# A hand-fixed instruction order for the recurrence preparation of a hybrid decoder layer

## The chip, the core and the metric

The kernel runs on one core of one Trainium2 chip. A core has a matmul engine (TensorE, PE in the profile, with PEld for its weight loads), three engines for element-wise work (VectorE or DVE, ScalarE or ACT, GpSimd or POOL), and a queue for transfers (SyncE or SP). ACT and POOL can also issue transfers, in line with their other instructions. Each engine works through its own list of instructions in order; engines wait for each other by semaphores. The metric is the device time in microseconds (us) of one execution; a kernel's time is the median of its runs.

## The reference

One decoder layer on x of 1024 tokens by 1024 features, all in fp32:

```python
h = rms_norm(x, norm1_g)
proj = h @ w_in
p_rwkv, p_sb, q_mem, gate_logits = jnp.split(proj, cut, axis=-1)
y_a = rwkv7_branch(p_rwkv, ...)      # token shift, delta-rule recurrence, group norm, bonus
y_b = stick_breaking_branch(p_sb, ...)
y_m = memory_branch(q_mem, mem, ...)
merged = sum over branches of sigmoid(gates) * (branch @ w_branch)
x = x + merged @ w_out
x = x + conv_ffn(x, ...)
```

The part that the change touches is the start of `rwkv7_branch`: a token shift `p + (prev - p) * mu` of each projected tile, and what the recurrence needs per head before its steps can be done in chunks of 64 tokens:

```python
a = sigmoid(a0 + al @ a2);  g = sigmoid(gl) @ g2
kk = k * k_k / max(norm(k * k_k), 1e-12)
k  = k * (1 + (a - 1) * k_a)
S  = S * w + (S @ -kk) (kk * a)^T + v k^T;   y = S @ r
bonus = sum(r * k * r_k) * v
y = (group_norm(y) + bonus) * g
```

## The kernel before

Every large product is taken as three matmuls of fp32r halves (a high part and the rest), `mm3`: high times high, high times low, low times high. The work is written as Python generators. `stream` yields the *filler*: one item for each 128 columns of a projection. An item (`shift_item`, L286 to L299) fetches its weight tile on SP (`wr`, L77), splits it on ACT (`wh`, L81) and POOL (`wl`, L82) one item ahead, and then does eight steps, one for each 128 rows of the input; a step is six matmuls into two PSUM banks of the tag `mm`. At the end of an item `shifted` (L240 to L250) does the token shift: a memset and two multiplications by the row norm on VectorE (L244, L246, which read the two banks), a scaling on ACT (L247), and the weighted sum on VectorE (L249). `settle` marks the finished tile in the fourth step of the next item.

`rwkv_prep(p, ...)` prepares two of the eight heads for the recurrence, p = 0 to 3. `weave` alternates: one step of the preparation, up to its next `yield`, then one step of the filler. So the list of PE's instructions is fixed by the code: `pinned` ties each matmul and transpose behind the instruction that was written before it on its engine. VectorE's, ACT's and POOL's instructions in the preparation are not tied before the change. A scheduler puts them in order by its own estimate of when they are ready; instructions of the preparation are given a higher priority than the filler.

In the order of the code, a preparation of the kernel before is: the two low-rank gates (L320, L321 on ACT), a scan (L330) and kp (L326) on VectorE; the sums of squares on PE, a maximum (L335), a power on POOL (L337) and its spread over a tile `ex` (L255); rk (L353); the transposes of v with their copies (L359) and four stores from ACT; the transposes of `ex` on PE and kk (L369), b (L370); `chain(0)`; the bonus products of `blk` and rk on PE with `bon` on VectorE (L429, L430) and the scaling of g on ACT (L432); `gram` for the first and second quarter; `chain(1)`; `turned(0)`; `gram` for the third and fourth quarter; `turned(1)`. `chain(h)` makes the operands of half h: four products with 64 partitions (L379, two with b and two with kp) and three instructions for `ra` (L380, L381, L382). `gram(h, f)` is 16 matmuls with 64 rows each into two banks, and two multiplications by a mask on VectorE that empty them (L396). `decayed(h)` (POOL, L408) scales half h, `turned(h)` transposes that on PE (L106), and ACT copies the result (L418). All these banks are of the tag `g`, of which there are four.

After the four preparations the filler goes on with the projections of the second branch. `differ` (L681) subtracts two tiles on VectorE four times; one tile of each comes back from memory, where it was stored just before. `inst` (L452, a transfer issued by POOL) loads what the Gram groups stored in `mad`, for `inverse`, which runs on VectorE in the stage after.

Of the kernel before, what the change touches and what calls it, by code (L numbers as in the profile page):

```python
# [50 lines left out]
class Trunk:  # L51
    def __init__(self, ctx, tc, I, out):
        self.ctx, self.tc, self.nc, self.I, self.out = ctx, tc, tc.nc, I, out
        self.uid = 0
        self.pin = False
# [52 lines left out]
    def pinned(self, ins):  # L108
        if self.pin:
            self.tc.keep_in_program_order(ins)  # L110

# [128 lines left out]
    def shifted(self, ti, tag, pp=None):  # L240
        nc = self.nc
        pp = pp or self.proj(self.I["w_in"][ti])
        pr, tmp = self.t4(), self.t4()
        nc.vector.memset(tmp[:, 0:1], 0.0)  # L244
        for h in range(2):
            nc.vector.tensor_tensor(pr[:, h * 512 : (h + 1) * 512], pp[h], self.rbc[:, h * 512 : (h + 1) * 512], ALU.mult)  # L246
        nc.scalar.activation(tmp[:, 1:1024], pr[:, 0:1023], AF.Copy, scale=self.par("mu", ti))  # L247
        out = self.t4(tag)
        nc.vector.scalar_tensor_tensor(out, pr, self.omm[:, ti : ti + 1], tmp, ALU.mult, ALU.add)  # L249
        return out  # L250

    def expand_heads(self, f, tag="w4"):
        nc = self.nc
        ex = self.t4(tag)
        nc.vector.tensor_copy(  # L255
            ex[:, :1024].rearrange("p (j h i) -> p j h i", j=8, h=2),
            f.rearrange("p (j h) -> p j h", j=8).unsqueeze(3).to_broadcast([128, 8, 2, 64]),
        )
        return ex
# [26 lines left out]
    def shift_item(self, ti, out, name):  # L286
# [18 lines left out]
    def rwkv_prep(self, p, krv, need):  # L305
# [3 lines left out]
        halves = [slice(0, 512), slice(512, 1024)]  # L309
        if p == 0:  # L310
# [5 lines left out]
        for hs in halves:  # L316
# [3 lines left out]
            nc.scalar.activation(a[:, hs], pa, AF.Sigmoid, bias=self.par("a0", p))  # L320
            nc.scalar.activation(su[:, hs], pu, AF.Sigmoid, bias=self.par("w0", p))  # L321
        P = self.t4("qk")
        nc.scalar.activation(P, k, AF.Square, scale=self.par("k_k", p))
        kp = self.t4("qk")
        nc.scalar.activation(kp, a, AF.Identity, scale=self.par("k_a", p), bias=self.omka[:, p : p + 1])
        nc.vector.tensor_tensor(kp, k, kp, ALU.mult)  # L326
        for _ in range(2):
            yield
        cc = Q = su
        nc.vector.tensor_tensor_scan(cc, self.seg, su, 0.0, ALU.mult, ALU.add)  # L330
        for _ in range(2):
            yield
        pst = self.head_ss(P)
        mx = self.small("rs", [128, 16])
        nc.vector.tensor_scalar(mx, pst, 1e-24, None, ALU.max)  # L335
# [3 lines left out]
        for hs in halves:  # L339
            pgh = self.ps("g")  # L340
            self.mmul(pgh, lora[:, 512 + p * 128 : 512 + (p + 1) * 128], self.sg[:, hs], start=True, stop=True)
            nc.scalar.activation(g[:, hs], pgh, AF.Copy)
        nc.scalar.activation(P, cc, AF.Exp, scale=-EXPM, bias=self.offs[:, 0:1])
        pc = self.pc[p]
        nc.scalar.activation(pc, cc.rearrange("p (c s) -> p c s", c=NC)[:, :, 63], AF.Exp, scale=-EXPM)
        nc.scalar.activation(Q, cc, AF.Exp, scale=EXPM, bias=self.offs[:, 1:2])
        ex = self.expand_heads(inv, "it")
        for _ in range(3):
            yield
        need(f"v{p}")  # L350
        r, v = krv[1], krv[2]
        rk = self.t4("qk")
        nc.vector.scalar_tensor_tensor(rk, r, self.par("r_k", p), kp, ALU.mult, ALU.mult)  # L353
        vt = self.t4("qk")
        for h, hs in enumerate(halves):
# [3 lines left out]
            nc.scalar.activation(vt[:, hs], pt, AF.Copy)  # L359
# [5 lines left out]
        for _ in range(2):  # L365
            yield
        kk, b = k, a
        for hs, bc in zip(halves, self.bcast_heads(ex)):
            nc.vector.scalar_tensor_tensor(kk[:, hs], k[:, hs], self.par("k_k", p), bc, ALU.mult, ALU.mult)  # L369
        nc.vector.tensor_tensor(b, kk, a, ALU.mult)  # L370

        def chain(h):
            hs = halves[h]
            bk, ra = self.t4("qk"), self.t4("qk")
            bk4, ra4 = (x.rearrange("p (c u s) -> p c u s", c=8, u=2) for x in (bk, ra))
            for x, first in ((b, 1), (kp, 0)):
                for h2 in range(2):
                    q = slice(h2 * 64, h2 * 64 + 64)
                    nc.vector.tensor_tensor(bk4[q, :, first ^ h2], self.c8(x[q, hs]), self.c8(Q[q, hs]), ALU.mult)  # L379
            nc.vector.tensor_tensor(ra4[:, :, 0], self.c8(r[:, hs]), self.c8(P[:, hs]), ALU.mult)  # L380
            nc.vector.scalar_tensor_tensor(ra4[:, :, 1, 1:64], self.c8(P[:, hs])[:, :, 0:63], -1.0, self.c8(kk[:, hs])[:, :, 1:64], ALU.mult, ALU.mult)  # L381
            nc.vector.tensor_scalar(ra4[:, :, 1, 0], self.c8(kk[:, hs])[:, :, 0], -math.exp(OFF), None, ALU.mult)  # L382
            self.spill(p, h, 0, ra, nc.sync)
            return bk, ra

        def gram(h, f, bk, ra):
            mt = self.t4("at")
            mt4 = mt.rearrange("p (c h t) -> p c h t", c=4, h=2)
            pm = [self.ps("g"), self.ps("g")]
            for c in range(4):  # L390
                o = (f * 4 + c) * 128
                for h2 in range(2):
                    q = slice(h2 * 64, h2 * 64 + 64)
                    self.mmul(pm[h2][:, c * 128 : (c + 1) * 128], bk[q, o : o + 128], ra[q, o : o + 128], start=True, stop=True)
            for h2 in range(2):
                nc.vector.tensor_tensor(  # L396
                    mt4[:, :, h2], pm[h2].rearrange("p (c t) -> p c t", c=4),
                    self.mm_mask.unsqueeze(1).to_broadcast([128, 4, 128]), ALU.mult)
            g0 = h * 4 + f * 2
            nc.sync.dma_start(  # L400
# [1540 lines left out]
```

## Time and profile before

| what | us |
|---|---|
| median of 3 runs | 1829.22 (1829.06 to 1833.78) |
| the profiled execution | 1831.78 |
| its span from first to last instruction | 1830.0 |
| PE busy in the span | 1785.9 (98%) |
| VectorE busy | 1191.1 (65%) |
| ACT busy | 881.9 (48%) |
| POOL busy | 771.2 (42%) |
| granted TensorE clock, mean | 0.995 |

Matmuls overlap, so that a matmul's own length in the profile (about 0.39 us for 512 columns) is longer than the distance between the starts of two. Distances are the better measure of what PE does. Idle time of PE is what the waits of PE add up to; idle time of another engine costs something only where PE waits for it in the end. The four preparations lie between 60 and 286 us of the span.

### The profile page before, as it was taken

What the parts mean: (1) busy time and instruction counts of PE and PEld (TensorE: products, weight loads), DVE (VectorE), ACT (ScalarE), POOL (GpSimd) and SP (SyncE); (2) the same over time, 40 slices, a digit from 0 to 9 for tenths busy, and PEclk for the clock granted to TensorE, in tenths of its full rate; (3) what the DMA queues carried; (4) which work ended last, traced back from release to release, by engine and by line L of the source; (5) the groups of instructions that cost most, each with busy time, mean ns of one, the idle gap of its engine ahead of it and who ended that gap; (6) DMA issues with size and microseconds to landing.
All of it is one profiled execution on the core that took longest, in us unless ns stands there. A gap on an engine that the chain in (4) does not pass through costs nothing.

```text
span 1830.0 us, 27430 instructions
## 1 busy us (share of the span) xinstructions
PE 1785.9 (98%) x10468; PEld 1445.7 (79%) x10468; DVE 1191.1 (65%) x1659; ACT 881.9 (48%) x1665; POOL 771.2 (42%) x441
## 2 busy tenths in 40 slices
PE   8999999999999999999899999989999999999999
PEld 6777778878788888787677878868888888888887
DVE  5657664988987514333444793597776777785497
ACT  5443342564666635534456443464454444545443
POOL 2322343232222452122233341376776767645454
PEclk9999999999999999999899999999999999999999
DMA  4255466111112351467665463323232232386475
GB/s 181 58 173 184 151 201 204 50 41 52 56 45 84 112 144 53 164 211 257 222 244 185 163 251 104 114 70 115 101 117 88 95 118 104 123 291 247 144 236 202
DMA packets 120613, 263.39 MB, mean 144 GB/s; under 512 B 28313, under 2 KB 40857, under 8 KB 120354
## 3 DMA queue, kind: packets, MB, share of 16 engines
q1 hardware_dynamic: 82722, 194.76, 32.6%
q10 hardware_dynamic: 33984, 54.27, 8.1%
q0 software_dynamic: 3776, 12.62, 2.2%
q8 instruction: 82, 1.34, 0.3%
q14 instruction: 49, 0.40, 0.1%
HBM read 180.04 MB, written 81.53 MB: 143 GB/s over the span
## 4 chain that ended last, share of the span: by engine, by line
PE 83%; DVE 8%; issue 3%; ACT 3%; POOL 2%; DMA 1%; ACTq 0%; SPq 0%; DVEq 0%; POOLq 0%
PE mm L113 67%; PE g L113 12%; PE g L106 3%; POOL dw L1677 1%; DVE qk L379 1%; DVE qk L381 1%; DVE it L462 1%; DVE BT L1318 1%; DVE inst L464 0%; DVE at L854 0%; DVE mg L1232 0%; DMA w<-yd 0%; ACT wh L81 0%; POOL wl L82 0%; DVE qk L382 0%
## 5 line engine op out<-in xcount | busy, mean ns | idle before, releaser
L82 POOL TENSOR_TENSOR wl<-wr,wh 128x1024 fp32r<-128x1024 f32 x77 | 196.8, 2557 | 473.4 <-ACT wh L81 469.7
L113 PE MATMUL mm<-xhi,wh 128*128 128x512 f32 x784 | 264.6, 418 | 9.4 <-ACT xhi L182 7.5
L113 PE MATMUL mm<-xlo,wh 128*128 128x512 f32 x784 | 245.8, 395 | 0.9 <-DVE xlo L183 0.9
L113 PE MATMUL mm<-xhi,wl 128*128 128x512 f32 x784 | 244.3, 393 | 0.3 <-POOL wl L82 0.2
L113 PEld LDWEIGHTS mm<-xlo,wh 128*128 128x128 f32 x784 | 148.8, 190 | 34.5 <-DVE xlo L183 1.6
L113 PEld LDWEIGHTS mm<-xhi,wl 128*128 128x128 f32 x784 | 148.3, 189 | 34.0 <-POOL wl L82 1.2
L113 PEld LDWEIGHTS mm<-xhi,wh 128*128 128x128 f32 x784 | 137.7, 191 | 39.5 <-issue 9.1
L81 ACT ACTIVATE wh<-wr 128x1024 fp32r<-128x1024 f32 x77 | 81.4, 1058 | 147.0 <-PE mm L113 85.4
L113 PE MATMUL mm<-dw,da 128*128 128x512 f32 x528 | 121.2, 390 | 0.0
L113 PE MATMUL mm<-BT,l 128*128 128x512 f32 x504 | 117.7, 390 | 0.0
L113 PEld LDWEIGHTS mm<-dw,da 128*128 128x128 f32 x528 | 99.0, 188 | 21.6 <-DVE da L1676 1.2
L1677 POOL TENSOR_TENSOR dw<-draw,dw 128x512 fp32r<-128x512 f32 x55 | 81.9, 1499 | 79.1 <-ACT dw L1675 76.4
L113 PE MATMUL mm<-BT,wh 128*128 128x512 f32 x352 | 109.2, 391 | 2.9 <-DVE BT L1318 2.9
L854 DVE TENSOR_TENSOR_SCAN at<-at,at 128x128 f32<-128x128 f32 (+3 forms) x64 | 93.4, 1460 | 26.6 <-ACT at L848 26.4
L113 PEld LDWEIGHTS mm<-BT,l 128*128 128x128 f32 x504 | 94.7, 188 | 19.6
L113 PE MATMUL mm<-B,wh 128*128 128x512 f32 x352 | 108.7, 390 | 1.5 <-DVE p L1508 1.5
L1676 DVE TENSOR_TENSOR da<-draw,da 128x512 fp32r<-128x512 f32 x77 | 67.0, 877 | 49.5 <-ACT da L1674 49.1
L1409 POOL TENSOR_TENSOR l<-it,l 128x1024 fp32r<-128x1024 f32 x21 | 51.6, 2458 | 95.5 <-ACT l L1408 95.5
L113 PE MATMUL g<-dw,da 128*128 128x512 f32 x396 | 90.6, 390 | 0.3 <-POOL dw L1677 0.3
L1674 ACT ACTIVATE da<-draw 128x512 fp32r<-128x512 f32 x77 | 48.3, 628 | 80.8 <-PE mm L113 30.9
L113 PEld LDWEIGHTS g<-dw,da 128*128 128x128 f32 x396 | 74.3, 188 | 16.1 <-POOL dw L1677 0.8
L756 DVE TENSOR_TENSOR w<-w,rbc 128x1024 f32<-128x1024 f32 x24 | 49.8, 2074 | 56.8 <-ACT w L755 55.0
(329 smaller groups left out, 3996.5 us busy)
## 6 DMA issues: line engine op xcount, KB each, us to landing
wr<-in_w_in_dram SPq DMA_DIRECT2D x50, 512.0 KB, 3.6
draw<-actd SPq DMA_DIRECT2D x77, 256.0 KB, 3.5
at<-scr SPq DMA_DIRECT2D x28, 512.0 KB, 5.8
draw<-in_w_down_dram SPq DMA_DIRECT2D x55, 256.0 KB, 4.7
rw<-in_w_up_dram SPq DMA_DIRECT2D x22, 512.0 KB, 3.5
actd<-gall ACTq DMA_DIRECT2D x44, 256.0 KB, 3.3
gsd<-w ACTq DMA_DIRECT2D x20, 512.0 KB, 2.8
wr<-in_w_up_dram SPq DMA_DIRECT2D x20, 512.0 KB, 3.6
```

The source lines that it names most:

```text
L81: self.nc.scalar.activation(hi, raw, AF.Copy)
L82: self.nc.gpsimd.tensor_tensor(lo, raw, hi.bitcast(F32), ALU.subtract)
L106: self.pinned(self.nc.tensor.transpose(out, in_, self.ident[:n, :n]))
L113: self.pinned(self.nc.tensor.matmul(*a, **k))
L379: nc.vector.tensor_tensor(bk4[q, :, first ^ h2], self.c8(x[q, hs]), self.c8(Q[q, hs]), ALU.mult)
L381: nc.vector.scalar_tensor_tensor(ra4[:, :, 1, 1:64], self.c8(P[:, hs])[:, :, 0:63], -1.0, self.c8(kk[:, hs])[:, :, 1:64], ALU.mult, ALU.mult)
L756: nc.vector.tensor_tensor(g, g, self.rbc, ALU.mult)
L854: self.pinned(nc.vector.tensor_tensor_scan(sn[:, :W][:, ::-1], sn[:, :W][:, ::-1], self.smask[:, 1024 - W :][:, ::-1], 1.0, ALU.mult, ALU. ...
L1409: keep(eng.tensor_tensor(lo, src, hi.bitcast(F32), ALU.subtract))
L1674: self.pinned(nc.scalar.activation(A[:, 0], a, AF.Copy))
L1676: self.pinned(nc.vector.tensor_tensor(A[:, 1], a, A[:, 0].bitcast(F32), ALU.subtract))
L1677: nc.gpsimd.tensor_tensor(Wt[:, 1], w, Wt[:, 0].bitcast(F32), ALU.subtract)
```

## The change

**A fixed order.** While the four preparations are woven, `strict` is set. Each pinned instruction is then tied behind the last pinned one of its engine, in addition to the instruction written directly before it. And far more is pinned: all of the preparation's VectorE and ACT instructions but those of `decayed` and the power on POOL, and the token shifts of the filler. Not pinned are the weight splits, the transfers, `differ`, and the copies of the third projection group on ACT (L661).

**Shifts in two steps.** The last instruction of a token shift (L249) is put aside in `tails` and written in the second step of the next item, after whatever the preparation has written by then.

**VectorE's work piece by piece.** In the new order a preparation has 28 steps (27 before), numbered s0 to s27 here:

- s0 gates on PE and ACT; s2 scan; s3 kp; s4 sums of squares on PE, maximum, power on POOL, g and the three exponentials on ACT; s7 `ex`
- s8 transposes of v, copies, four stores from ACT, rk; s10 transposes of `ex` *and* the four bonus products on PE in one run, kk; s11 b
- s12 `ra` of half 0 and its store; s13 the two products with b; s14 the two with kp; s15 `decayed(0)`, the two `bon` multiplications; s16 the last `bon` step, the scaling of g, their stores
- s17 all 32 matmuls of `gram(0)` in one run, masks of the first quarter; s18 masks of the second quarter
- s19 `ra` of half 1; s20 `turned(0)`, products with b; s21 products with kp; s22 `decayed(1)`
- s24 all 32 matmuls of `gram(1)`, masks; s25 masks; s27 `turned(1)` and the load of `inst`

Before, all of kk, b and `chain(0)` were one step, and `chain(1)` was written together with the second `gram`. The four banks of the tag `g` are all taken in s10 (two for `ex`, two for the bonus, which are read in s10 and s15) and again in s17 and s24.

The core of the diff:

```diff
     def pinned(self, ins):
         if self.pin:
             self.tc.keep_in_program_order(ins)
+            if self.strict:
+                self.behind(ins, self.last_fixed.get(ins.ins.engine))
+            self.last_fixed[ins.ins.engine] = ins
+        return ins
...
     def shifted(self, ti, tag, pp=None):
...
+        finish = lambda: self.pinned(nc.vector.scalar_tensor_tensor(out, pr, self.omm[:, ti : ti + 1], tmp, ALU.mult, ALU.add))
+        if self.pin:
+            self.tails.append(finish)
...
     def shift_item(self, ti, out, name):
...
-            if k == 3:
+            if k == 1:
+                self.finish_tails()
+            elif k == 3:
                 self.settle()
...
+        bcs = self.bcast_heads(ex)
+        pbs = []
+        for hs in halves:
+            pbs.append(self.ps("g"))
+            self.mmul(pbs[-1], self.blk, rk[:, hs], start=True, stop=True)
+        for hs, bc in zip(halves, bcs):
+            stt(kk[:, hs], k[:, hs], self.par("k_k", p), bc, ALU.mult, ALU.mult)
+        yield
+        tt(b, kk, a, ALU.mult)
+        yield
...
+        def gram(h, bk, ra):
+            pms = []
+            for f in range(2):
+                pm = [self.ps("g"), self.ps("g")]
+                for c in range(4):
...
+                pms.append(pm)
+            for f, pm in enumerate(pms):
...
+                    tt(mt4[:, :, h2], pm[h2].rearrange("p (c t) -> p c t", c=4),
+                       self.mm_mask.unsqueeze(1).to_broadcast([128, 4, 128]), ALU.mult)
...
+                yield
...
+        self.strict = True
         for p in range(4):
             self.weave(self.rwkv_prep(p, krv[p], need), pump, 1.0)
+        self.strict = False
```

More of the change, by code (lines that the diff above doesn't have):

```diff
@@ L54, in __init__ @@
         self.uid = 0
-        self.pin = False
+        self.pin = self.strict = False
+        self.last_fixed, self.tails = {}, []
     def nm(self, s):
@@ L110, in pinned, with behind @@
             self.tc.keep_in_program_order(ins)
+            if self.strict:
+                self.behind(ins, self.last_fixed.get(ins.ins.engine))
+            self.last_fixed[ins.ins.engine] = ins
+        return ins
+    def behind(self, ins, prev):
+        if prev is not None:
+            self.tc.add_manual_dep(
+                ins.ins, prev.ins.name,
+                mybir.DependencyInfo(mybir.DependencyClass.NoSync, mybir.DependencyReason.DATA), reason="fixed order")
     def mmul(self, *a, **k):
@@ L258, in expand_heads @@
         )
+        if tag == "it":
+            self.pinned(ins)
         return ex
@@ L383, in chain @@
[L383 to L391, printed above, removed]
-                for h2 in range(2):
[L393 to L400, printed above, removed]
-                self.scr[p, g0 : g0 + 2, :, 512:1024].rearrange("g q c -> q g c"), mt.rearrange("q (g c) -> q g c", g=2))
-            for h2 in range(2):
-                i0 = p * 32 + h2 * 16 + h * 8 + f * 4
-                nc.sync.dma_start(self.mad[i0 : i0 + 4].rearrange("c s t -> s c t"), mt4[64 - h2 * 64 : 128 - h2 * 64, :, h2, 64:128])
+                    tt(bk4[q, :, first ^ h2], self.c8(x[q, hs]), self.c8(Q[q, hs]), ALU.mult)
@@ L665, in item @@
                         self.raw.append(raw)
-                if i == 1:
+                if i == 0:
+                    self.finish_tails()
+                elif i == 1:
                     self.settle()
```

133 lines of the change are left out of this document (74 added, 59 removed).

## The prediction

> **What bounds the kernel now.** I read the page first, then busy time by stage, then PE's waits in the stage that is touched, then the timeline around one of them.
>
> ```profile
> span 1830.0 us, 27430 instructions
> PE 1785.9 (98%) x10468; PEld 1445.7 (79%) x10468; DVE 1191.1 (65%) x1659; ACT 881.9 (48%) x1665; POOL 771.2 (42%) x441
> PE 83%; DVE 8%; issue 3%; ACT 3%; POOL 2%; DMA 1%; ACTq 0%; SPq 0%; DVEq 0%; POOLq 0%
> ```
>
> PE sets the time: 98% busy, and 83% of the chain that ended last. Only two things can move it: fewer waits of PE, and less time of PE itself. A window over the four preparations shows how much there is (busy us and instructions of PE, PEld, DVE, ACT, POOL, then clock, transfer share and rate):
>
> ```profile
> 60.00:286.00 226.00, 216.77 (x1243) 166.48 (x1242) 150.53 (x177) 90.33 (x111) 76.80 (x34) 0.99 0.52 166
> ```
>
> PE idles 226 - 216.8 = 9.2 us there, and VectorE is busy for two thirds of it, so it is not full on average. The waits of PE from 60 to 330 us name the cause:
>
> ```profile
> PE g L106 <- DVE at L396: 6.4, 3, 2.6
> PE g L113 <- DVE qk L382: 2.4, 2, 1.8
> PE g L106 <- DVE at L249: 0.4, 1, 0.4
> ```
>
> The largest is `turned(0)`, which needs a bank that the masks of the first Gram groups (L396) must empty. PE's and VectorE's timeline around the first of the three (start, length, then idle before):
>
> ```profile
> 93.27 0.61 PE L113 MATMUL mm<-xhi,wl 128*128 128x512 f32 x2
> 93.82 1.16 PE L113 MATMUL g<-qk,qk 64*128 64x128 f32 x16
> 94.91 0.73 PE L113 MATMUL mm<-xhi,wh 128*128 128x512 f32 x2
> 95.48 0.63 PE L113 MATMUL mm<-xlo,wh 128*128 128x512 f32 x2
> 98.63 0.62 PE L113 MATMUL mm<-xhi,wl 128*128 128x512 f32 x2
> 100.01 0.62 PE L113 MATMUL mm<-xhi,wl 128*128 128x512 f32 x2
> 102.89 1.16 PE L106 MATMUL g<-kon,it 128*128 128x128 f32 x8 [2.26 <-DVE at L396]
> ```
>
> ```profile
> 97.68 0.69 DVE L380 TENSOR_TENSOR qk<-at,qk 128x512 f32<-128x512 f32 x1
> 98.29 0.68 DVE L381 SCALAR_TENSOR_TENSOR qk<-qk,at 128x504 f32<-128x504 f32 x1
> 98.88 0.17 DVE L382 TENSOR_SCALAR qk<-at 128x8 f32<-128x8 f32 x1
> 100.86 1.29 DVE L249 SCALAR_TENSOR_TENSOR at<-w,omm,w 128x1024 f32<-128x1024 f32 x1 [1.21 <-ACT w L247]
> 102.06 2.48 DVE L396 TENSOR_TENSOR at<-g,kon 128x512 f32<-128x512 f32 x4
> ```
>
> The first Gram group was in its banks at 95.0. Its masks begin at 102.06, 7 us later, behind all of `chain(1)`, a token shift, and 1.21 us in which VectorE waits for ACT in that shift. So the wait is one of order and not of load.
>
> **The change, part by part.** Lengths of VectorE's instructions are means over 60 to 330 us (count, busy us, mean ns, idle before):
>
> ```profile
> L379 DVE TENSOR_TENSOR qk<-qk,qk 64x512 f32<-64x512 f32 x32 | 21.9, 684 | 0.5
> L396 DVE TENSOR_TENSOR at<-g,kon 128x512 f32<-128x512 f32 x32 | 20.1, 680 | 5.9 <-PE g L113 5.9
> L249 DVE SCALAR_TENSOR_TENSOR at<-w,omm,w 128x1024 f32<-128x1024 f32 x11 | 19.6, 1781 | 10.8 <-ACT w L247 10.8
> L246 DVE TENSOR_TENSOR w<-mm,rbc 128x512 f32<-128x512 f32 x22 | 14.2, 684 | 12.3 <-PE mm L113 12.2
> L381 DVE SCALAR_TENSOR_TENSOR qk<-qk,at 128x504 f32<-128x504 f32 x8 | 13.5, 1681 | 0.0
> L380 DVE TENSOR_TENSOR qk<-at,qk 128x512 f32<-128x512 f32 x8 | 8.4, 1044 | 0.2
> L382 DVE TENSOR_SCALAR qk<-at 128x8 f32<-128x8 f32 x8 | 5.7, 714 | 0.0
> L369 DVE SCALAR_TENSOR_TENSOR at<-at,params,g 128x512 f32<-128x512 f32 x8 | 5.6, 745 | 4.8 <-PE g L106 4.7
> L429 DVE TENSOR_TENSOR at<-g,at 128x512 f32<-128x512 f32 x8 | 5.4, 682 | 0.1
> L430 DVE SCALAR_TENSOR_TENSOR at<-at,params,qk 128x1024 f32<-128x1024 f32 x4 | 5.1, 1272 | 0.0
> L370 DVE TENSOR_TENSOR qk<-at,qk 128x1024 f32<-128x1024 f32 x4 | 4.9, 1225 | 0.1
> ```
>
> *(1) The old waits go: -9.2 us.* The masks now stand ahead of `chain(1)` and ahead of the next token shift, and the shift's last step stands two filler steps after ACT's scaling, so the 10.8 us before L249 go too. What is late next comes under (3) to (5).
>
> *(2) Gram groups of a half: -3.2 us.* A filler step of six matmuls takes 1.38 us (98.63 to 100.01), so two take 0.46. From 93.27 to 95.48 are four of them (0.92 us) and one Gram group, which thus takes 1.29 us: eight pairs side by side, 128 columns wide. The nearest run of eight at full rows is `turned(1)`:
>
> ```profile
> 117.03 0.62 PE L113 MATMUL mm<-xhi,wl 128*128 128x512 f32 x2
> 118.83 0.62 PE L113 MATMUL mm<-xlo,wh 128*128 128x512 f32 x2
> ```
>
> Eight transposes of 128 columns and four matmuls lie between these starts, so the transposes take 1.80 - 0.92 = 0.88 us. The other 0.41 us of a Gram group is for going into 64 rows and out. Eight such passages fall away: 8 x 0.4 = 3.2. Low end: only the visible edges, 0.09 us before 93.82 (93.27 + 0.46 = 93.73) and 0.11 us too much from 94.91 to 95.48, which is 0.2 x 8 = 1.6. I take the upper end, since width and count are alike. The bonus products were in one step already and have full rows; I cost their move at nothing on PE, bounds 0 and -0.8 (four passages at 0.2).
>
> *(3) A new wait before `gram(0)`: +4.4 us.* Filler items end every eighth step. Preparation 0 starts after six steps and waits in s8 for the mark of v0 (step 20); the others follow each 28 steps. So an item ends after s11 and s19 in preparations 0 and 2, after s7, s15 and s23 in 1, and 3 has no token shifts. In 0 and 2 VectorE now cannot go on with `ra` before PE has finished that item. From there PE has five filler steps to s17: 6.9 us. VectorE has L246 twice (1.37), `ra` (1.68 + 0.71 + 1.04 = 3.43), b products (1.37), the put-aside L249 (1.78), kp products (1.37): 9.3 us by the means. Where nothing disturbs it, `ra` takes 0.68 + 0.17 + 0.69 = 1.54 and L249 1.29 (timeline above): 6.9 us. The first quarter waits 0 to 2.4 us; the second also needs the bonus banks, whose two L429 take 1.36 against 0.9 of matmuls: 0.5 more. So 0.5 to 2.9 us, twice. What disturbs is POOL:
>
> ```profile
> 89.66 2.84 POOL L82 TENSOR_TENSOR wl<-wr,wh 128x1024 fp32r<-128x1024 f32 x1
> 90.18 2.87 DVE L381 SCALAR_TENSOR_TENSOR qk<-qk,at 128x504 f32<-128x504 f32 x1
> ```
>
> L381 needs 2.87 us beside the weight split and 0.68 us without. The next split becomes possible when an item ends, so one falls into this window; I take 2.2 us for each, 4.4 in all (ends 1.0 and 5.8). [...] In 1 and 3, from the transposes of `ex` on, VectorE needs kk (1.49), b (1.23), `ra` 3.43 and four products (2.74), 8.9 us, while PE has seven steps (9.7 us) and the bonus products, 1.9 us a preparation by this row:
>
> ```profile
> L113 PE MATMUL g<-qk,kon 128*128 128x512 f32 x16 | 7.5, 592 | 0.0
> ```
>
> No wait there. rk, which PE now needs in s10, is written two steps earlier; the slack is 2.8 us plus 1.8 us of transposes.
>
> *(4) `gram(1)`: +0.6 us.* From the end of the bonus reads to s24 PE has half a group (1.0), seven steps (9.7) and eight transposes (0.9): 11.6 us. VectorE has L430 (1.27), four masks (2.72), `ra` 3.43, four products 2.74, one L246 pair 1.37: 11.5. Level by the means; one more meeting with POOL (2.2 us) would show in one of three. Ends 0 and 3.
>
> *(5) The end of preparation 3: +0.5 us.* `differ` is written between s24 and s25. So the last two masks come behind its fourth subtraction, which waits for stored tiles (60 to 345 us):
>
> ```profile
> DVE A L681 <- DMA A<-vsd: 23.9, 3, 10.3
> POOL inst L452 <- DMA mad<-at: 10.8, 2, 9.8
> ```
>
> VectorE stands there for up to 10.3 us, and with it the store of `mad`, the load of `inst` on POOL's queue and SP's queue behind the masks. `turned(1)` uses the banks of the first quarter, which are free; PE needs no other bank of that tag for some 16 filler steps. Ends 0 and 3; the case beyond is a rival.
>
> ACT's fixed order: its scaling of g (L432) waits for VectorE and holds what follows on ACT, the next token shift's scaling and store among it. It had to wait there before too, and PE's waits show none for it; the cover is that weights are split one item ahead (8 x 1.38 = 11 us, of which POOL's part takes 2.84 in the row above). I cost it at nothing; were that cover gone, PE would wait as long as L430 is late, 1 to 2 us a preparation. The spill of `ra` on SP comes earlier: nothing.
>
> Sum: -9.2 - 3.2 + 4.4 + 0.6 + 0.5 = -6.9 us, from the profiled 1831.78 to 1824.9. The median of the runs lies 2.56 us under the profiled execution, so 1822.3.
>
> **Rivals.** *The waits only move.* All of (3) to (5) at their upper ends, 5.8 + 3 + 3 = 11.8, leaves -0.6 us: 1828.6. For it: in s17 to s24 (4) finds VectorE level with PE, and in (3) it is late by the means. Against: it no longer loses the time before L249, and 1 and 3 have room.
>
> *Slower: POOL's queue at the end of preparation 3.* If the load of `inst` is queued ahead of the next weight split, POOL stands until the masks, the store of `mad` and its landing are done. The fourth subtraction ended 16 us after the last copy (L661) of what it reads:
>
> ```profile
> 284.96 0.69 ACT L661 ACTIVATE at<-mm,rsc 128x512 f32<-128x512 f32 x1 [0.67 <-PE mm L113]
> 300.57 1.23 DVE L681 TENSOR_TENSOR A<-A,at 128x1024 f32<-128x1024 f32 x1 [4.47 <-DMA A<-vsd]
> mad<-at SPq DMA_DIRECT2D x32, 64.0 KB, 3.5
> ```
>
> With two masks (1.4), the store of `mad` (3.5) and the split (2.8) that makes 23.8 us. PE wants the split after `gram(1)`, `turned(1)` and one item, 2.1 + 0.9 + 11.0 = 14 us: a wait of 9.8 us, 1832, and each us of further lateness adds one. It costs the whole forecast gain from 7 us on, and is over 0.3% from 12.5 us, where the subtraction comes 3 us later still; ACT, held before the store that it reads, could do that. For it: the 9.8 us above. Against: before, the split behind it came in time. [...]
>
> **How the numbers follow.** A change of 0.3% (5.5 us) is about what can be told from none. The forecast has 0.57, its own range 1817 to 1826 by the ends of (2) to (5), not all at once; the waits that only move 0.24; POOL's queue 0.19. Faster by over 0.3%, under 1823.7, is most of the first and none of the others: 0.51. Within 0.3%: the rest of the first, the second and a quarter of the third, 0.34. Slower: 0.15. The range from 1815 to 1832.5 leaves out the later part of the third case and a little below.
>
> **What would show it.** Right: no wait for L396 in PE's waits; Gram groups of 32; a wait of 1 to 3 us before the first and third `gram(0)`, on L379 or L429; VectorE idle before L246 and not before L249. Wrong: waits of PE over 9 us from 60 to 286; PE waiting for `wl` after the fourth preparation.

## The result, and the profile after

| | median of 20 runs, us | range |
|---|---|---|
| before | 1831.69 | 1829.06 to 1834.14 |
| after | 1827.78 | 1822.91 to 1831.47 |

The ratio is 0.9977, 95% interval 0.9971 to 0.9983: 3.9 us less, 0.2%, where 9.4 us were forecast against this median (1831.69 to 1822.3). The median of three runs that the prediction started from, 1829.22, was low by 2.5 us; the profiled execution (1831.78) had been close to the middle, and should have been left as the base.

The changed kernel's span, its busy times, and the shares of the chain that ended last:

```profile
span 1827.0 us, 27450 instructions
PE 1783.8 (98%) x10468; PEld 1447.8 (79%) x10468; DVE 1189.1 (65%) x1659; ACT 881.9 (48%) x1665; POOL 773.1 (42%) x441
PE 69%; DVE 7%; issue 3%; ACT 2%; POOL 1%; DMA 1%; SPq 0%; DVEq 0%; POOLq 0%; ACTq 0%
```

PE still sets the time, and its busy time fell by only 2.1 us. The waits of PE from 60 to 345 us in the new kernel (total, times, longest):

```profile
PE g L124 <- DVE qk L334: 5.6, 9, 2.2
PE g L107 <- DVE at L891: 1.6, 1, 1.6
PE g L107 <- DVE w L274: 1.1, 1, 1.1
```

The 9.2 us of before are gone with their lines, and 8.3 us stand here under new ones. (L334 and L335 are the pinned multiplications of the helper; L124 and L107 are the matmul and the transpose, L113 and L106 before.) The first line consists of waits before `gram`. PE's timeline around the first, the third and the fourth `gram(0)`:

```profile
96.03 0.46 PE L124 MATMUL g<-qk,qk 64*128 64x128 f32 x2 [0.93 <-DVE qk L334]
96.75 2.38 PE L124 MATMUL g<-qk,qk 64*128 64x128 f32 x30 [0.26 <-DVE qk L334]
...
204.15 0.46 PE L124 MATMUL g<-qk,qk 64*128 64x128 f32 x2 [0.93 <-DVE qk L334]
...
261.37 0.46 PE L124 MATMUL g<-qk,qk 64*128 64x128 f32 x2 [2.24 <-DVE qk L334]
262.09 0.69 PE L124 MATMUL g<-qk,qk 64*128 64x128 f32 x6 [0.26 <-DVE qk L334]
```

Preparations 0 and 2 wait 1.2 us each (0.93 + 0.26: one kp product and then the other). Preparation 1 does not wait. Preparation 3, for which the prediction had no wait, has the longest. VectorE's timeline ahead of it says why:

```profile
247.45 1.41 DVE L335 SCALAR_TENSOR_TENSOR at<-at,params,g 128x512 f32<-128x512 f32 x2 [2.65 <-PE g L107]
253.87 2.95 DVE L718 TENSOR_TENSOR A<-A,w 128x1024 f32<-128x1024 f32 x1 [5.02 <-DMA A<-vsd]
256.74 1.21 DVE L334 TENSOR_TENSOR qk<-at,qk 128x1024 f32<-128x1024 f32 x1
...
261.97 1.29 DVE L334 TENSOR_TENSOR at<-g,at 128x512 f32<-128x512 f32 x2
263.18 1.82 DVE L718 TENSOR_TENSOR A<-A,w 128x1024 f32<-128x1024 f32 x1
```

L718 is the first subtraction of `differ`. It isn't pinned, and the scheduler put it between kk (247.45) and b (256.74), in s10, while the code has it after s24. There it waited 5.0 us for a transfer, took 2.95, and everything for `gram(0)` stood behind it. Its second one stands in the middle of `bon`, between the two multiplications and the last step. The other two stand ahead of the last masks, as the code has them:

```profile
278.02 1.29 DVE L334 TENSOR_TENSOR at<-g,kon 128x512 f32<-128x512 f32 x2 [1.12 <-PE g L124]
287.18 1.23 DVE L718 TENSOR_TENSOR A<-A,at 128x1024 f32<-128x1024 f32 x1 [7.87 <-DMA A<-vsd]
291.37 1.23 DVE L718 TENSOR_TENSOR A<-A,at 128x1024 f32<-128x1024 f32 x1 [2.96 <-DMA A<-vsd]
292.51 1.28 DVE L334 TENSOR_TENSOR at<-g,kon 128x512 f32<-128x512 f32 x2
303.14 2.03 DVE L497 TENSOR_TENSOR it<-inst 128x62 f32<-128x62 f32 x1 [9.34 <-DMA inst<-mad]
...
307.18 0.17 DVE L738 TENSOR_TENSOR hn<-g,rsc 128x16 f32<-128x16 f32 x1
```

So the inverse begins at 303.1 (301.7 before). VectorE's queue holds its first steps ahead of the head norm (L738), and the norm is late against PE: its copy (L274) starts 8.4 us after PE's sums for the norm (302.90 and 311.32), where the kernel before needs 7.1 (308.53 and 315.66). PE waits 1.1 us for this copy. The scan (L891) starts 26.9 us after the copy, and PE waits 1.6 us for it; how much of that is the inverse's doing is asked again under (5) below.

The joined Gram matmuls where nothing is waited for, in preparation 1:

```profile
149.64 0.61 PE L124 MATMUL mm<-xhi,wl 128*128 128x512 f32 x2
150.18 2.06 PE L124 MATMUL g<-qk,qk 64*128 64x128 f32 x32
152.17 0.73 PE L124 MATMUL mm<-xhi,wh 128*128 128x512 f32 x2
152.74 0.62 PE L124 MATMUL mm<-xlo,wh 128*128 128x512 f32 x2
```

From 149.64 to 152.74 are four filler matmuls (0.92) and all 32 of a half: 2.18 us, where two groups took 2 x 1.29. That is 0.4 us for each of eight halves, 3.2 us. With the waits the account gives 9.2 - 8.3 + 3.2 = 4.1 us, and 3.9 were measured. That they meet is in part luck. From 60 to 345 us the profiled execution of before has two stretches of 3.4 us at half the granted clock (at 153 and 310 us), that of the changed kernel one (at 262 us), and the sum leaves them out, though such a stretch costs PE 1.6 us where the rows show it (see the last section).

### The profile page after: what moved, and what is told of

The parts are those of the page before. It is cut to its first block, busy times and chain, and to the rows that moved or that the text cites. A ratio compares the mean times of both kernels' runs of the same rounds, so it can differ in the third digit from the quotient of the medians.

```text
span 1827.0 us, 27450 instructions
## 1 busy us (share of the span) xinstructions
PE 1783.8 (98%) x10468; PEld 1447.8 (79%) x10468; DVE 1189.1 (65%) x1659; ACT 881.9 (48%) x1665; POOL 773.1 (42%) x441
## 4 chain that ended last, share of the span: by engine, by line
PE 69%; DVE 7%; issue 3%; ACT 2%; POOL 1%; DMA 1%; SPq 0%; DVEq 0%; POOLq 0%; ACTq 0%
PE mm L124 58%; PE g L124 9%; PE g L107 3%; POOL dw L1714 1%; DVE it L497 1%; DVE inst L499 1%; DVE at L891 1%; DVE BT L1355 1%; DVE qk L838 0%; DVE qk L837 0%; DVE mg L1269 0%; DMA w<-yd 0%; DMA at<-gsd 0%; DMA wr<-in_w_in_dram 0%; DVE at L1257 0%
## 5 line engine op out<-in xcount | busy, mean ns | idle before, releaser
L124 PE MATMUL mm<-xhi,wh 128*128 128x512 f32 x784 | 262.9, 416 | 9.3 <-ACT xhi L193 7.3
L124 PE MATMUL mm<-xlo,wh 128*128 128x512 f32 x784 | 244.9, 394 | 0.9 <-DVE xlo L194 0.9
L124 PE MATMUL mm<-xhi,wl 128*128 128x512 f32 x784 | 243.2, 392 | 0.3 <-POOL wl L83 0.3
L124 PEld LDWEIGHTS mm<-xlo,wh 128*128 128x128 f32 x784 | 148.0, 189 | 34.3 <-DVE xlo L194 1.6
L124 PEld LDWEIGHTS mm<-xhi,wl 128*128 128x128 f32 x784 | 147.7, 189 | 33.5 <-POOL wl L83 0.9
L124 PEld LDWEIGHTS mm<-xhi,wh 128*128 128x128 f32 x784 | 138.2, 191 | 39.5 <-issue 9.1
L124 PE MATMUL mm<-dw,da 128*128 128x512 f32 x528 | 120.8, 390 | 0.0
L124 PE MATMUL mm<-BT,l 128*128 128x512 f32 x504 | 117.7, 389 | 0.0
L124 PEld LDWEIGHTS mm<-dw,da 128*128 128x128 f32 x528 | 99.0, 188 | 21.2 <-DVE da L1713 0.8
L124 PE MATMUL mm<-BT,wh 128*128 128x512 f32 x352 | 109.1, 390 | 2.9 <-DVE BT L1355 2.9
L124 PEld LDWEIGHTS mm<-BT,l 128*128 128x128 f32 x504 | 94.6, 188 | 19.6
L124 PE MATMUL mm<-B,wh 128*128 128x512 f32 x352 | 108.6, 390 | 1.5 <-DVE p L1545 1.5
L891 DVE TENSOR_TENSOR_SCAN at<-at,at 128x128 f32<-128x128 f32 (+3 forms) x64 | 88.7, 1391 | 28.0 <-ACT at L885 28.0
L124 PE MATMUL g<-dw,da 128*128 128x512 f32 x396 | 90.5, 390 | 0.4 <-POOL dw L1714 0.4
L124 PEld LDWEIGHTS g<-dw,da 128*128 128x128 f32 x396 | 74.3, 188 | 16.1 <-POOL dw L1714 0.8
```

The source lines that it names most:

```text
L124: self.pinned(self.nc.tensor.matmul(*a, **k))
L891: self.pinned(nc.vector.tensor_tensor_scan(sn[:, :W][:, ::-1], sn[:, :W][:, ::-1], self.smask[:, 1024 - W :][:, ::-1], 1.0, ALU.mult, ALU. ...
```

## The experiments

My theory after the result: the order written out is right, and what is lost is `differ`, which was left out of it. Rivals: the tie itself (`strict`) costs or gains something; the joining gains less than its matmuls show; preparations 0 and 2 are the larger loss. Each experiment has the kernel before on the same chip beside it (medians 1831.4 to 1831.7).

**`differ` fixed in its place.**

```diff
-            nc.vector.tensor_tensor(v, v, raw, ALU.subtract)
+            self.pinned(nc.vector.tensor_tensor(v, v, raw, ALU.subtract))
```

> The changed kernel, with the four subtractions of differ pinned where they are written (between s24 and s25 of preparation 3), so that none of them can be queued between kk and b. Theory: the 2.2 us that PE waits before gram(0) of preparation 3 are the first subtraction, which stands 5.0 us for its transfer in front of b. Then that wait falls under 0.5 us, the waits after the preparations (L274 and the scan of the attention, 1.1 + 1.6 us) stay, and the time is 2 to 3 us under the changed kernel (ratio to before 0.996 to 0.997). Rival: VectorE is full in preparation 3, since weights are split every 5.5 us there; the wait stays at 1.5 us or more and the ratio at 0.9977.

Measured: 1822.7 us (1819.12 to 1823.27), ratio 0.9945 (0.9933 to 0.9958), 5 us under the changed kernel and outside its interval, where 2 to 3 us were expected. VectorE's timeline at the same place, and PE's waits from 60 to 345 us:

```profile
249.07 1.41 DVE L335 SCALAR_TENSOR_TENSOR at<-at,params,g 128x512 f32<-128x512 f32 x2 [2.65 <-PE g L107]
250.51 1.22 DVE L334 TENSOR_TENSOR qk<-at,qk 128x1024 f32<-128x1024 f32 x1
251.66 0.68 DVE L335 SCALAR_TENSOR_TENSOR qk<-qk,at 128x504 f32<-128x504 f32 x1
```

```profile
PE g L124 <- DVE qk L334: 2.8, 6, 0.9
PE mm L124 <- POOL wl L83: 1.3, 1, 1.3
```

b follows kk at once, and the wait of 2.24 us is gone. A wait of 1.3 us for a weight split is new at 261 us: `decayed(0)` comes earlier on POOL (255.87) and now stands ahead of the split, whose part on ACT was done at 254.9. The two waits after the preparations, which I had expected to stay, are gone too. The waits are 4.1 us in place of 8.3, but this is not yet an account of the 5 us. PE's sums for the head norm and the transposes that need L274, in the changed kernel and then in this one:

```profile
302.90 1.10 PE L124 MATMUL g<-kon,w 128*64 128x2 f32 x32
312.16 1.06 PE L107 MATMUL g<-kon,w 128*128 128x128 f32 x8 [1.14 <-DVE w L274]
```

```profile
300.81 1.10 PE L124 MATMUL g<-kon,w 128*64 128x2 f32 x32
310.39 1.03 PE L107 MATMUL g<-kon,w 128*128 128x128 f32 x8
```

At the sums PE is 2.1 us ahead, with one stretch at half clock behind it in either execution; so much the preparations give. The inverse began at 299.1, L274 follows the sums by 6.9 us in place of 8.4, and the wait for it goes. For the scan this trace can't tell: from 303.2 to 306.7 PE ran at half clock (two filler matmuls start 0.85 us apart there and 0.45 outside), so the transposes came 9.6 us after the sums, where they come after 8.0 without such a stretch (303.38 and 311.35 in the last experiment). What PE did not wait there it lost to the clock. Two later kernels with the same edit have no such stretch at that place, and both waits.

**`differ` later.** As the last one, and called from the fourth step of the item behind it:

```diff
-            items += [*([self.differ] if p == 0 else []), kp, gate(), *([self.spread_last] if p == 0 else []), kss, qp, gate(hooks), mark(f"sb{p}")]
+            items += [kp, gate(), *([self.spread_last] if p == 0 else []), kss, qp, gate(hooks), mark(f"sb{p}")]
...
-        return self.proj_item(w[18 + p], k_fin), k_ss, self.proj_item(w[14 + p], q_fin, kq), hooks
+        return self.proj_item(w[18 + p], k_fin, {4: self.differ} if p == 0 else {}), k_ss, self.proj_item(w[14 + p], q_fin, kq), hooks
```

> As the run before, and differ is written five filler steps later, behind the last masks of preparation 3. Theory: the last masks, the store of mad and the load of inst no longer wait for differ; inverse begins about 10 us earlier, and the two waits of PE after the preparations, 2.7 us, go as well: 5 us under the changed kernel, ratio 0.994 to 0.9955. Rival: those two waits come from the order of inverse and the head norms on VectorE whatever the load of inst does; then the ratio is that of the run before.

Measured: 1826.13 us (1823.94 to 1828.42), ratio 0.9967 (0.9955 to 0.9979). In the preparations it waits as the kernel above does (2.7 and 1.3 us). What it loses lies at 722 us, in the memory attention: PE waits 4.3 us for L1074, and 1.2 in the changed kernel. ACT's timeline shows what stands ahead:

```profile
716.65 1.06 ACT L82 ACTIVATE wh<-wr 128x1024 fp32r<-128x1024 f32 x1 [6.73 <-PE mm L124]
717.62 0.55 ACT L1110 ACTIVATE at<-g,nb,hf 128x256 f32<-128x256 f32 x1
```

A weight split, which is not pinned there, was placed ahead of the exponentials and waited 6.7 us. In the changed kernel the same split stands behind them (722.02). Moving four subtractions probably gave the scheduler other estimates, so that it ordered other free work differently 430 us on; that reason was not tested. This run tells of that and not of where `differ` is best.

**Without the tie.** `strict` stays off, the rest of the change stands:

```diff
-        self.strict = True
+        self.strict = False
```

> The changed kernel with the new order of the code and everything pinned as in it, but without the tie behind the last pinned instruction of the engine. Theory that the fixed order itself is what removed the old waits: masks and subtractions drift again, PE waits 7 to 10 us in the preparations, ratio 0.998 to 1.000. Rival, that giving the work out in pieces is enough: waits of 4 to 6 us as in the changed kernel, ratio within 0.0007 of 0.9977.

Measured: 1827.98 us (1826.01 to 1831.21), ratio 0.9978 (0.9969 to 0.9987), the same as the changed kernel. PE waits 5.1 us for L334 and 1.3 for L891, and L718 stands between kk and b here too. What the change gains it gains by its written order and by pinning, which were not tried apart; the additional tie is worth nothing that can be measured.

**Gram groups of a quarter again.**

```diff
-            pms = []
             for f in range(2):
...
-                pms.append(pm)
-            for f, pm in enumerate(pms):
```

> The changed kernel with the Gram matmuls in groups of a quarter again, one in each of the two steps. If the two edges of a group cost 0.4 us, eight more groups cost 3.1 us: ratio 0.9992 to 0.9996. If the edges are hidden in the waits before gram(0), where PE stands for VectorE anyway, it is less: the second quarter comes 1.4 us later, and the 0.5 us for the bonus banks go; ratio 0.998 to 0.999.

Measured: 1829.47 us (1827.84 to 1832.61), ratio 0.9988 (0.9979 to 0.9997). The difference of the ratios, 0.0011, is 2.0 us. PE's waits are 7.6 us against 8.3, so 0.7 of the 3.2 us that the joins save is paid in waits, and 2.5 are left by the rows.

**The joins alone, in the kernel before.** Its `gram` was rewritten as in the change, with its masks in the two steps in which they were.

```diff
-        gram(0, 0, *u0)
-        yield
-        gram(0, 1, *u0)
+        yield from gram(0, *u0)
```

> The kernel before with one part of the change alone: the 32 Gram matmuls of a half in one run, the masks behind them in two steps as they were. Theory of the prediction (0.4 us for each of 8 joins): -3 us, to 1828.7, if the waits of the old order stay as they are. Rival: in the old order the second quarter's matmuls now need their inputs an item earlier or the masks come as late as before, so the waits for the masks (6.4 us) grow by what the join saves; within 1 us of 1831.7.

Measured: 1828.76 us (1826.27 to 1832.67), ratio 0.9991 (0.9982 to 0.9999). By medians that is 2.6 us, by the ratio 1.6. The waits for the masks grew from 6.4 to 7.7 us: the theory's 3 us less 1.3, a part of the rival. PE also waits 1.6 us for the scan (L856 here), as in the changed kernel for L891, though the inverse started at 300.0 in this execution. The kernel before shows no such wait, but its profiled execution ran at half clock from 309.8 to 313.2 us, between the sums and the transposes (9.6 us apart, 8.0 here).

**`differ` fixed in the kernel before.** The same edit as the first, at L681.

> The kernel before with nothing changed but differ's four subtractions fixed in place. In the kernel before, the first of them stood, without a wait of its own, 1.2 us ahead of the masks for which PE then waited 2.6 us at 270 us. Theory, the free subtraction costs what it puts in front of PE's next need, and in the old order that is only its own 1.2 us: -1.0 to -1.5 us, to 1830.4 with the masks' wait at 1.3 us. Rival, its place cost the old order nothing, since the masks' wait was for VectorE's whole queue: within 0.5 us of 1831.7. A third: as much as in the new order (-5 us), which would mean that fixing these four is worth the same in any order.

Measured: 1829.39 us (1828.05 to 1832.59), ratio 0.9994 (0.9986 to 1.0003), which the times can't tell from no change. In the trace the waits for the masks fell from 6.4 to 5.2 us, by the 1.2 us of the one subtraction that had stood ahead of them. The third case, 5 us in any order, is excluded: the same four instructions cost the new order far more, since there they stood with their transfer wait ahead of b.

**Shift in one step again,** on the base of the first experiment:

```diff
-        if self.pin:
-            self.tails.append(finish)
-        else:
-            finish()
+        finish()
```

> The same base (differ's subtractions in place, 1822.7 us) with the token shift in one step again: its last multiply-add stands straight behind the two products and waits for ScalarE's copy. Theory, the two-step shift is worth something only where VectorE is last: VectorE idles about 1.2 us before each L260 once more, and PE's waits in 60 to 345 us grow from 4.1 to 6 - 9 us; the time rises by 1.5 to 4 us. Rival, the idle time only changes place (VectorE waits for the projection in any case): PE's waits stay within 1 us of 4.1, the time within 0.5 us of 1822.7.

Measured: 1824.98 us (1822.58 to 1827.4), ratio 0.9966 (0.9956 to 0.9976), 2.3 us slower than its base, with intervals that just touch. VectorE's groups for L260 from 60 to 330 us, first in this kernel and then in its base:

```profile
L260 DVE SCALAR_TENSOR_TENSOR at<-w,omm,w 128x1024 f32<-128x1024 f32 x11 | 21.6, 1968 | 13.9 <-ACT w L258 13.9
```

```profile
L260 DVE SCALAR_TENSOR_TENSOR at<-w,omm,w 128x1024 f32<-128x1024 f32 x11 | 15.9, 1446 | 3.7 <-ACT w L258 3.6
```

Ten us more of VectorE standing idle cost PE 1.1 us before a bonus product; the waits after the preparations (1.6 + 0.4 us) are there too, with the inverse started at 302.4. PE's waits are 7.2 us against 4.1. The theory's numbers hold, but two thirds of the growth lie where it did not look for them, and these 2.0 us can't be laid to the edit: in its base a stretch at half clock stood at that place.

**The kp products of half 0 earlier,** on the base of the first experiment: behind rk, in s9, in place of s14.

```diff
+        u0, u1 = [self.t4("qk")], []
+        products(0, u0[0], kp, 0)
         yield
...
-            for x, first in ((b, 1), (kp, 0)):
+            products(h, bk, b, 1)
+            yield
+            if h:
+                products(h, bk, kp, 0)
```

> The new kernel with differ's four subtractions fixed in place (the first experiment, 1822.7 us) and, in each preparation, the kp products of the first half moved from the end of its item to just behind rk, one item earlier. Theory: PE's waits of 0.9 + 0.26 us before the first and the third gram(0) are set by VectorE, whose last item before them starts only when the gate's product has come (it is idle 2.0 us until then) and holds 8.1 us of work; taking the 1.4 us of the kp products out of it is more than the 0.9 us that are waited. PE's waits for L334 go from 2.8 to 1.0 us or less, and the time falls by 1.5 to 2.5 us, to 1820.2 - 1821.2. Rival, the wait only moves: what the products displace in the earlier item (the normalised keys, b) comes later and PE waits as long for the first ra or for the shift; the time stays within 0.5 us of 1822.7 and the 2.8 us stand, under another line.

Measured: 1821.36 us (1820.02 to 1825.6), ratio 0.9955 (0.9939 to 0.997), which cannot be told from its base. The waits for L334 on `qk` fell from 2.8 to 0.4 us, but PE now waits 1.5 us before the second quarter, twice. PE's timeline, VectorE's and POOL's at the first of the two:

```profile
96.13 1.16 PE L124 MATMUL g<-qk,qk 64*128 64x128 f32 x16
98.82 1.75 PE L124 MATMUL g<-qk,qk 64*128 64x128 f32 x16 [1.53 <-DVE at L334]
```

```profile
95.14 3.02 DVE L260 SCALAR_TENSOR_TENSOR at<-w,omm,w 128x1024 f32<-128x1024 f32 x1
98.08 1.28 DVE L334 TENSOR_TENSOR at<-g,at 128x512 f32<-128x512 f32 x2
```

```profile
95.19 1.90 POOL L460 TENSOR_TENSOR it<-qk,pc 128x1024 f32<-128x1024 f32 x1 [2.62 <-DVE qk L334]
```

`decayed(0)` on POOL follows the products, so it came earlier too, and fell on the put-aside end of a shift: 3.02 us beside it, 1.28 in the changed kernel. The `bon` multiplications, which empty the second pair of banks, came late by that much. After the preparations PE waits 1.6 + 1.1 us, as in the changed kernel. The rival was right in its mechanism: the wait moved. The time lies between the two forecasts and decides for neither.

**`differ`'s subtractions behind the last masks,** on the base of the first experiment, its loads where they were:

```diff
-            self.pinned(nc.vector.tensor_tensor(v, v, raw, ALU.subtract))
+            self.diffs.append((v, raw))
...
         yield from gram(1, *u1)
+        for x, raw in self.diffs if p == 3 else []:
+            tt(x, x, raw, ALU.subtract)
```

> The new kernel with differ's loads where they are and its four subtractions, in fixed order, moved behind the last Gram masks of preparation 3 (in the first experiment they were fixed ahead of them: 1822.7 us, where the last masks stood until 288.2 us behind a subtraction that waited 3.9 us for its transfer, and the inverse's first operation ran at 299.1). Theory: what is left of differ's cost is that the inverse's load follows the last masks; they run right after their matmuls, at about 280 - 284 us, the inverse starts at 292 - 296 us, the subtractions lie in VectorE's idle time before it, and no wait for L274 or L891 stands after the preparations in any run. PE's waits in 60 to 345 us stay at or under 4.1 us; time 1821 - 1822.7. Rival, PE does not wait there any more in the first experiment, so nothing is left to gain, and the subtractions' reads hold their buffers longer: a new wait of POOL or of a projection for a buffer, 1823 - 1826.

Measured: 1821.62 us (1820.72 to 1823.6), ratio 0.9945 (0.9933 to 0.9958), as its base. VectorE's timeline:

```profile
276.87 2.49 DVE L334 TENSOR_TENSOR at<-g,kon 128x512 f32<-128x512 f32 x4 [6.19 <-PE g L124]
...
291.12 2.88 DVE L334 TENSOR_TENSOR A<-A,at 128x1024 f32<-128x1024 f32 x1 [6.29 <-DMA A<-vsd]
295.21 0.23 DVE L499 TENSOR_TENSOR it<-inst 128x62 f32<-128x62 f32 x1 [1.21 <-DMA inst<-mad]
...
301.68 0.19 DVE L732 COPY jk<-g 128x32 f32<-128x32 f32 x1 [3.22 <-PE g L124]
```

The masks end at 279, the inverse starts 4 us earlier than in the base and 8 earlier than in the changed kernel, and the copy ahead of the head norm (L732) now waits for PE and not in VectorE's queue. The time shows no gain, as the rival said, and the new waits that it feared did not come. Why there is none the traces leave open: this execution, like that of the base, ran at half clock just there (302.8 to 306.3 us), so neither shows whether PE would have waited.

**Both.** The early products and the subtractions behind the masks.

> The same with the kp products of the first half one item earlier (the experiment on the early products, 1821.4 us, whose profiled execution still waited 1.5 us for the masks once, 0.4 us for the inputs of Gram groups, and 1.6 + 1.1 us after the preparations for L902 and L274). Theory: the two waits after the preparations are the inverse's late start, so they go: PE's waits in 60 to 345 us fall from 6.2 to about 3.5 us and the time by 1 to 2.7 us, to 1818.7 - 1820.4, the fastest of all. Rival: those waits come from the head norm's own chain (column sums, GpSimd's power, the expansion), which the inverse does not feed; they stay, and the time is within 0.7 us of 1821.4.

Measured: 1820.33 us (1815.82 to 1824.43), ratio 0.9937 (0.9923 to 0.9951). The wait for L274 is gone, and that of 1.6 us for the scan is 1.0; the inverse started at 298.5. There is no stretch at half clock at that place here. This is the lowest median, 11 us under the kernel before, though its interval overlaps those of the first experiment, the early products and the subtractions behind the masks. PE's waits fell from 6.2 to 4.4 us, the theory's way and half as far; whether any of the 1 us against the early products alone is real the times can't tell.

## Why the prediction was right and wrong

*(1) The old waits go, -9.2:* right; no line of them is left. *(2) Groups of a half, -3.2:* right, 3.2 by the rows; the experiments on it left 1.6 to 2.6 us in the time, because some of it is paid back in waits.

*(3) The wait before `gram(0)`, +4.4:* its mechanism and place were right for preparations 0 and 2, the size was 1.2 us each and not 2.2. POOL's split did make L335 2.7 us long there, but the put-aside L260 took 1.28 and not the mean of 1.78, and no wait for the bonus banks came, for which 0.5 stood. VectorE's timeline ahead of the first `gram(0)` in the changed kernel, and POOL's two instructions in that stretch:

```profile
89.32 2.69 DVE L335 SCALAR_TENSOR_TENSOR qk<-qk,at 128x504 f32<-128x504 f32 x1
...
94.00 1.28 DVE L260 SCALAR_TENSOR_TENSOR at<-w,omm,w 128x1024 f32<-128x1024 f32 x1
...
96.63 1.29 DVE L334 TENSOR_TENSOR at<-g,at 128x512 f32<-128x512 f32 x2
```

```profile
89.07 2.40 POOL L83 TENSOR_TENSOR wl<-wr,wh 128x1024 fp32r<-128x1024 f32 x1 [11.70 <-ACT wh L82]
96.68 1.90 POOL L448 TENSOR_TENSOR it<-qk,pc 128x1024 f32<-128x1024 f32 x1 [5.21 <-DVE qk L334]
```

"No wait" held for preparation 1 and failed for 3, and this is the first failed step: 2.5 us, because I treated `differ` as work with a place "between s24 and s25". That is where the code has it. It is not pinned, so the order gave it no place at all, and the scheduler put it into s10. The section on the change lists it among what is not pinned.

*(4) `gram(1)`, +0.6:* the rows show 0.15 + 0.26 us in preparation 2 and 0.26 in 3, 0.7 in all.

*(5) The end of preparation 3, +0.5:* the second failed step; the rows show 2.7 us, near its upper end. The place was right (last masks behind the fourth subtraction, store of `mad`, load of `inst`), the one who suffers was not. I followed the delay to the banks and to POOL's queue, and left out that VectorE itself has the inverse's first steps queued ahead of the head norm, for which PE waits next. That is shown for the 1.1 us of L274: where the norm is not held, L274 follows PE's sums by 6.4 or 6.5 us (the last two experiments) and not by 8.4. The 1.6 us for the scan are the inverse's only in part. 1.0 is left where the norm isn't held and the clock is full (both edits together), and 1.6 came in the old order too, with the joins alone. The kernel before should show it as well, by these rows, had its clock not been halved there; no run shows how much of it is the change's. POOL's queue, the slower rival, did no harm: the split that I feared behind the load of `inst` ran ahead of it, as POOL's timeline in the changed kernel shows:

```profile
291.84 3.03 POOL L83 TENSOR_TENSOR wl<-wr,wh 128x1024 fp32r<-128x1024 f32 x1 [9.73 <-ACT wh L82]
297.73 0.60 POOL L487 DMA_DIRECT2D inst<-mad  x1 [2.86 <-DMA mad<-at]
```

ACT's fixed order, put at nothing, cost nothing: in the changed kernel PE waits for no weight split from 60 to 345 us.

Together: (3) 4.9 in place of 4.4, (4) 0.7 in place of 0.6, (5) 2.7 in place of 0.5. The sum is then -4.1 and not -6.9, which from the profiled 1831.78 makes 1827.7 (the clock left out, as said above); the last 2.6 us between 1822.3 and 1824.9 were the wrong base. The two entries in which `differ` stands, 2.5 and 2.7 us, are 5.2 us, and fixing it gave 5.0; that they agree is in part luck as well. The first is sure: in the new order the wait of 2.24 us was gone in all six kernels in which `differ` is fixed or moved, and stood in the three in which it is free (2.23 or 2.24 us each). But 1.3 us for a weight split came in its place in four of the six. The second is not: where `differ` was fixed in the same place and the clock at the head norm was full, 2.0 and 2.7 us still stood there (inverse at 302.4 and 302.9); with its subtractions behind the masks and a full clock 1.0 was left (298.5). So these waits hang on when the inverse starts, and with that on the transfer ahead of the last masks, and on the clock, more than on the pinning. Of the 5 us that fixing `differ` gave, 2.1 are seen up to the head norm; the rest is not taken apart. "The waits only move" asked for 11.8 us of new waits; 8.3 came, about midway between that and the 5.5 of the forecast.

The signs listed beforehand came as said: no wait for L396, groups of 32, no wait of PE for `wl` after the fourth preparation. VectorE's idle time before L260 was 3.7 us where L249 had 10.8: most of it went, not all.

How VectorE fares beside GpSimd shows again in the early products' rows: L260 took 3.02 us beside `decayed(0)`, which is its 1.28 and nearly all of `decayed`'s 1.90. Not every meeting cost as much. In the changed kernel `decayed(0)` (L448, 96.68 to 98.58) ran beside the two `bon` multiplications at 96.63, which take one input from a bank, and those took 1.29 us for both, against 1.28 in the early products, where they ran after it. The last `bon` step began at 97.96, within `decayed(0)`, and took 1.70 us in place of the 1.28 of the early products. By these rows `decayed(0)` cost VectorE about 0.4 us at its place in the changed kernel, and 1.7 at the earlier one.

## What to carry to other kernels

When an order is pinned, the instructions left free are the ones to list and to follow: ask of each where the scheduler may put it and what it waits for, since a free instruction with a transfer wait can hold the pinned ones behind it, as L718 did here with its 5.0 us. Follow a delayed instruction also along its own engine's queue, to the next thing that the bounding engine needs, and not only to the buffers. Shifting work ahead carries along what follows it on other engines; here `decayed(0)` fell beside a VectorE instruction (3.02 us in place of 1.28), and new waits took the place of the old. And before two traces are compared wait by wait, look at the granted clock in the same window: a stretch at half clock can stand where a wait would be, and the wait then looks as if it were removed, as in the first experiment (303.2 to 306.7 us), where two later kernels with the same edit waited 1.1 + 1.6 and 0.4 + 1.6 us.

## What the hardware did that was not expected

The granted clock fell to half for stretches of 3.4 us. In the profiled execution of the changed kernel they begin at 262.4, 614.0 and 870.0 us, and at 890.4 one of twice that length; in that of the kernel before at 152.8, 309.8 and 873.0, and at 893.4 one of twice that length. A window view of the changed kernel (from:to, length, busy and count of PE, PEld, DVE, ACT, POOL, then clock, transfer share and rate), with the clock in the third column from the end:

```profile
614.00:617.40 3.40, 3.40 (x12) 2.66 (x11) 3.40 (x3) 1.54 (x3) 2.72 (x3) 0.51 0.00 0
617.40:620.00 2.60, 2.60 (x16) 2.25 (x15) 1.26 (x1) 1.48 (x3) 0.64 (x1) 0.99 0.52 150
866.00:870.00 4.00, 1.43 (x31) 1.08 (x32) 0.25 (x2) 3.61 (x16) 0.36 (x1) 1.00 0.90 292
870.00:873.40 3.40, 3.40 (x16) 2.61 (x13) 1.68 (x5) 0.00 (x0) 2.93 (x1) 0.51 0.45 183
```

PE was busy throughout both slow stretches. What one costs shows at the head norm: with a stretch between PE's sums and the transposes these lie 9.6 us apart (the kernel before, the first experiment), without one 8.0 (both edits together). That is 1.6 us, as much as most of the waits in this case. The second stretch follows one in which PE was busy for 1.43 of 4.0 us; the kernel before has it too, from 873.0, after 1.44 of 4.0 us, but none at 614. The mean clocks of the changed kernel's runs go from 0.993, in the run of 1831.47 us, to 0.999, in that of 1822.91, so this is a good part of the scatter, though runs at 0.995 alone go from 1825.48 to 1829.76, and small differences need several runs. For the stretch at 614 no idle time shows: PE's records are busy ahead of it, with 64 matmuls one column wide (611.06 to 613.1 us). Near 300 to 310 us stand matmuls two and four columns wide; a stretch follows them in the kernel before (309.8), in the first experiment (303.2) and with the subtractions behind the masks (302.8), and none does in the changed kernel, with the shift in one step and with both edits together. What brings a stretch on is not shown. At one place it stands behind a long wait: in the changed kernel a stretch at half clock begins at 262.4 us, about 1 us after the end of the wait of 2.24 us, and the two other kernels with that wait have one at that place, while the six without it have none from 258 to 290 us. The kernel before waits 2.56 us there without one, so no run shows this as a rule.
